# Adding Strassen sums to the residual by accumulating DMAs, in a transformer block on one Trainium2 core

## The chip, the core and the metric

The kernel runs on one NeuronCore of a Trainium2 chip. The core has five engines with an instruction queue each: TensorE (PE, matrix products; its weight loads are shown as PEld), VectorE (DVE), ScalarE (ACT), GpSimd (POOL) and SyncE (SP, which here only issues DMAs). An engine takes its instructions in order; what has to wait for another engine or for a DMA waits on a semaphore. Sixteen DMA engines carry all transfers. The metric is the device time of one execution in microseconds; it is the median of several runs.

## The reference, cut to what matters

One layer of an encoder block with four residual sub-blocks, each closed by a layer norm. 256 positions, 2048 features, everything in float32:

```python
h = layer_norm(ALPHA*h + 0.5*swiglu_ffn(h, ffn1_w_in, ffn1_w_out), ...)
h = layer_norm(ALPHA*h + hybrid_mixer(h, ...), ...)
h = layer_norm(ALPHA*h + memory_cross_attention(h, mem, ...), ...)
h = layer_norm(ALPHA*h + 0.5*swiglu_ffn(h, ffn2_w_in, ffn2_w_out), ...)
```

`ALPHA` is the fourth root of 2. The hidden width of an FFN is 5504. What matters here is the last product of a sub-block (`ffn1_w_out`, `w_xo`, `ffn2_w_out`), whose result, 256 x 2048, is added to `ALPHA*h`.

## The kernel before

**Arithmetic.** TensorE multiplies in a shorter float format. Each float32 operand is therefore split into a high plane (`hi`, ScalarE's copy, L264 for weights) and a remainder (`lo`, VectorE's subtraction, L267), and a product is the sum of three: high times high, remainder times high, high times remainder.

**Units.** Weights arrive in units of 1 MB in a `raw` buffer (three of them, loads issued by SP in L193, one by one as buffers come free). A unit holds two slices of 128 rows (contraction) of a group of 1024 output columns. `run` walks over a list of items; before an item's function is called it issues the loads and the splits (`load`, `halves`) of the units that come next, so the splits of later units stand ahead of the item's own instructions. Two pairs of `hi` and `lo` buffers exist.

**Groups.** `pair_group` computes 256 x 1024 outputs as 2 x 2 blocks of 128 x 512 in four PSUM banks `ps` (`mm` or `at`). A plain unit (`mm_pair`, L311) takes 24 matmuls. Some units, those in `at`, are done as a Strassen step (`mm_sums`, L366): seven block products in place of eight, 21 matmuls. They need sums of the weight blocks (`weight_sums`, L248 and L250, VectorE), sums of the activation blocks (`forms_step`, `sum_forms`, L321 and L325, VectorE), and four more banks `qs`. After the last such unit `shared` (the method, L679 to L684) combines the four banks into four sums of 128 x 512 in SBUF, tiles `w` (`w2`, six buffers, used by many steps): two copies on ScalarE and four additions on VectorE.

**Output groups.** `out_pair` is a group whose result goes to the residual `h`, two tiles of 128 x 2048. Right behind the method `shared`, its own inner function `shared` adds the four sums to `h`, on VectorE, with `ALPHA` multiplied in (L629) in the groups with `scale`, and without (L631) in the others. After the last unit `finish` adds the four banks `ps` (L754) and, where `st` is given, takes the layer norm's statistics of each piece (L390).

Seven output groups have Strassen steps: in ffn1 and in ffn2 each two of the first half of the hidden width (twelve units, Strassen steps in units 3, 5, 7 and 9, with `scale`) and one of the second half (ten units, the last a short one, steps in 3, 5 and 7, without `scale`, with statistics), and one in cross attention (eight units, steps in 2, 4 and 6, with `scale` and statistics). The remaining output columns are done by `out_proj` (L298) without Strassen steps. The two output groups of the mixer have none either; there `at` is empty and `finish` scales.

**Order.** `collect` gathers a stage's items into a list and `weave` puts side steps ahead of the list's entries by their position. In the first half of an FFN the side steps are: 2 the transposing DMAs of the last hidden block, 4 the sum forms of unit 7, 6 the return of that hidden block and the sum forms of unit 9. In cross attention: 1 the outputs of the last two heads and the forms of unit 2, 2 the forms of unit 4, 4 the forms of unit 6. Within this order the framework's scheduler decides how the instructions stand on each engine, by priority and readiness.

**GpSimd's queue** carries a few small loads: the gate bias rows (L912), the relative bias (L1048), rotation tables, the norm's gain and bias rows (L459, L460), the memory tokens (L1340, L1342).

Of the kernel before, what the change touches and what calls it, by code (L numbers as in the profile page):

```python
# [14 lines left out]
ALU = mybir.AluOpType  # L15
# [26 lines left out]
SUM_HOME = ("X2", "X3"),  # L42
# [5 lines left out]
ALPHA = 2.0 ** 0.25  # L48
# [53 lines left out]
class Kernel:  # L102
# [513 lines left out]
            turn = None  # L616
            f0 += nf

    def out_pair(self, bank, src, g, nk, x, at, fx, scale, st, sums_in=SUM_HOME):

        nc, h = self.nc, self.h
        ps, qs = {}, {}

        def shared():
            for (tt, a), s in qs["add"].items():
                c = (2 * g + a) * 512
                hs = h[tt][:, c:c + 512]
                if scale:
                    nc.vector.scalar_tensor_tensor(hs, hs, ALPHA, s, ALU.mult, ALU.add)  # L629
                else:  # L630
                    nc.vector.tensor_tensor(hs, hs, s, ALU.add)  # L631

        def finish():
            for tt in range(2):
                for a in range(2):
                    self.finish(tt, 2 * g + a, ps[tt, a], scale and not at, st)
        self.pair_group(bank, src, 512, nk, x, at, fx, ps, qs, shared, sums_in)
        self.add(finish)

    def group_tile(self, j):  # L640
# [1136 lines left out]
```

## Time and profile before

| | |
|---|---|
| median of 3 runs | 2434.71 us (2432.69 to 2434.84) |
| profiled execution, its time | 2432.52 us |
| profiled execution, its span | 2430.7 us |
| granted TensorE clock | 1.0 |
| instructions | 29702 |

A row of instructions reads: line of the kernel, engine, operation, output tile and input tiles (buffer numbers left out), shapes, and count. Where a row begins with two numbers, they are the start in the span and the duration, both in microseconds, and merged instructions of one kind carry a count (`x3`). Where it ends in three numbers with slashes, these are minimum, median and maximum of one instruction in nanoseconds. Rows of stretches give the busy time of each engine between two moments of the span, the number of instructions in brackets, then the clock, the share of the DMA engines' time and GB/s. DMA rows give the size of one transfer and the median time from its issue to its landing. Matmuls overlap one another, so a matmul's duration is longer than its share of TensorE's time.

### The profile page before, as it was taken

The page shows a single profiled execution, that of the slowest core. Times are in us where ns is not written, and L with a number is a line of the kernel's source. Part 1 is how long each engine was busy: PE and PEld are TensorE (multiplying, and loading weights), DVE is VectorE, ACT ScalarE, POOL GpSimd, SP SyncE. Part 2 cuts the span into 40 slices and gives each one's busy share as a digit, 9 for nine tenths or more (in the row PEclk, how much of TensorE's full clock was granted, in tenths as well). Part 3 has the DMA queues.
Part 4 walks back from the last instruction along what each step waited for, and adds up shares of the span by engine and source line. Part 5 has one row for each costly group of instructions (what it writes and reads, how often), then busy time and mean ns, then how long its engine had stood idle before and what let it go on. Part 6 is the DMA issues. An engine that isn't in the chain of part 4 may idle for free.

```text
span 2430.7 us, 29702 instructions
## 1 busy us (share of the span) xinstructions
PE 2422.3 (100%) x11280; PEld 2022.8 (83%) x11280; DVE 2130.9 (88%) x2437; ACT 1553.2 (64%) x2022; POOL 35.9 (1%) x81
## 2 busy tenths in 40 slices
PE   9999999999999999999999999999999999999999
PEld 8888888888888888888888888888888888888887
DVE  8999989899889998779788889979879999888997
ACT  6676745666555557878565687765666675556662
POOL 0000000000000001000000000000000000000000
PEclk9999999999999999999999999999999999999999
DMA  7766656667656657776577577655556766666665
GB/s 268 252 212 214 207 200 222 210 201 219 224 176 215 216 195 248 229 210 176 183 246 256 167 241 213 220 181 192 190 199 214 229 221 210 220 207 207 200 220 182
DMA packets 176414, 516.20 MB, mean 212 GB/s; under 512 B 111728, under 2 KB 112496, under 8 KB 121104
## 3 DMA queue, kind: packets, MB, share of 16 engines
q1 hardware_dynamic: 170816, 495.83, 61.6%
q0 software_dynamic: 4592, 17.30, 2.2%
q8 instruction: 88, 1.44, 0.2%
q10 hardware_dynamic: 864, 1.18, 0.1%
q14 instruction: 54, 0.44, 0.1%
HBM read 485.30 MB, written 2.10 MB: 201 GB/s over the span
## 4 chain that ended last, share of the span: by engine, by line
PE 89%; DVE 4%; ACT 3%; DMA 1%; issue 1%; SPq 0%; DVEq 0%; ACTq 0%
PE at L311 24%; PE mm L311 23%; PE at L366 11%; PE mm L366 11%; PE mm L298 10%; PE mm L277 4%; PE mm L279 2%; DVE lo L267 2%; ACT hi L264 1%; PE at L1034 1%; PE at L1505 0%; PE at L277 0%; DMA raw<-w_xv 0%; PE at L1088 0%; ACT H L854 0%
## 5 line engine op out<-in xcount | busy, mean ns | idle before, releaser
L264 ACT CAST hi<-raw 128x1024 fp32r<-128x1024 f32 (+1 forms) x852 | 804.0, 981 | 458.0 <-PE at L311 150.1
L267 DVE TENSOR_TENSOR lo<-raw,hi 128x2048 fp32r<-128x2048 f32 (+1 forms) x427 | 902.0, 2114 | 134.8 <-ACT hi L264 129.0
L311 PE MATMUL mm<-hi,T 128*128 128x512 f32 (+1 forms) x1312 | 307.5, 384 | 0.8 <-DVE v L400 0.7
L311 PEld LDWEIGHTS mm<-hi,T 128*128 128x128 f32 x1312 | 244.5, 188 | 46.9 <-DVE v L400 1.1
L264 ACT CAST X<-H 128x1024 fp32r<-128x1024 f32 (+1 forms) x170 | 174.8, 1035 | 160.9 <-DVE H L248 119.9
L311 PE MATMUL at<-hi,T 128*128 128x512 f32 x1136 | 272.3, 390 | 0.0
L311 PEld LDWEIGHTS at<-hi,T 128*128 128x128 f32 x1136 | 213.3, 188 | 44.5
L267 DVE TENSOR_TENSOR X<-H,X 128x2048 fp32r<-128x2048 f32 (+1 forms) x85 | 191.4, 2252 | 64.7 <-ACT X L264 64.7
L311 PE MATMUL mm<-lo,T 128*128 128x512 f32 (+1 forms) x656 | 158.4, 383 | 0.0
L311 PE MATMUL at<-lo,T 128*128 128x512 f32 x568 | 141.0, 389 | 0.0
L311 PEld LDWEIGHTS mm<-lo,T 128*128 128x128 f32 x656 | 122.3, 188 | 22.4
L311 PE MATMUL at<-hi,H 128*128 128x512 f32 x560 | 133.8, 390 | 0.0
L311 PEld LDWEIGHTS at<-lo,T 128*128 128x128 f32 x568 | 106.7, 188 | 22.1
L311 PEld LDWEIGHTS at<-hi,H 128*128 128x128 f32 x560 | 105.0, 188 | 21.5
L250 DVE TENSOR_TENSOR H<-H,raw 128x512 f32<-128x512 f32 (+1 forms) x170 | 115.4, 679 | 2.2
L311 PE MATMUL mm<-hi,H 128*128 128x512 f32 x480 | 115.5, 392 | 0.1
L311 PEld LDWEIGHTS mm<-hi,H 128*128 128x128 f32 x480 | 89.6, 188 | 18.9 <-DVE w L684 0.5
L248 DVE TENSOR_TENSOR H<-raw 128x1024 f32<-128x1024 f32 (+1 forms) x85 | 102.1, 1201 | 0.6 <-DMA raw<-w_gate 0.4
L366 PE MATMUL mm<-X,X 128*128 128x512 f32 x342 | 91.4, 393 | 0.0
L264 ACT CAST X<-raw 128x1024 fp32r<-128x1024 f32 (+1 forms) x54 | 55.4, 1035 | 47.9 <-DVE raw L250 38.6
L366 PE MATMUL at<-X,X 128*128 128x512 f32 (+1 forms) x315 | 82.6, 386 | 0.7 <-ACT X L264 0.7
L854 ACT COPY w<-w 128x1024 uint16<-128x1024 uint16 (+1 forms) x60 | 75.7, 1275 | 1.4 <-DMA w<-w 1.4
(387 smaller groups left out, 4151.3 us busy)
## 6 DMA issues: line engine op xcount, KB each, us to landing
raw<-ffn_w_in SPq DMA_DIRECT2D x150, 1024.0 KB, 4.9
raw<-ffn_w_out SPq DMA_DIRECT2D x66, 1024.0 KB, 4.9
raw<-w_gate SPq DMA_DIRECT2D x32, 1024.0 KB, 4.8
raw<-ffn_w_out_r SPq DMA_DIRECT2D x16, 1024.0 KB, 4.9
raw<-w_qk SPq DMA_DIRECT2D x16, 1024.0 KB, 5.6
raw<-w_o_b SPq DMA_DIRECT2D x16, 1024.0 KB, 4.8
raw<-w_out SPq DMA_DIRECT2D x16, 1024.0 KB, 5.0
raw<-w_xk SPq DMA_DIRECT2D x16, 1024.0 KB, 5.4
```

The source lines that it names most:

```text
L248: self.nc.vector.tensor_tensor(two[0], two[1], raw[:, :m].unsqueeze(1).to_broadcast([P, 2, m]), ALU.add)
L250: self.nc.vector.tensor_tensor(t[:, a * m:a * m + m], t[:, b * m:b * m + m], raw[:, a * m:a * m + m], ALU.add)
L264: self.last_hi = self.nc.scalar.copy(hi[:, c:d], src[:, c:d])
L267: self.last_lo = self.nc.vector.tensor_tensor(lo[:, :n], src, hi[:, :n].bitcast(F32), ALU.subtract)
L277: self.nc.tensor.matmul(ps, hi[j], x.both(kt), start=(j == 0), stop=False)
L279: self.last_mm = self.nc.tensor.matmul(ps[:, :S], lo[j], x.at(0, kt), start=False, stop=(j == n - 1))
L298: self.last_mm = self.nc.tensor.matmul(ps, x.at(xi, kt)[:, tt * P:(tt + 1) * P], w[wi][:, j * 512 + c:j * 512 + c + m], start=(start and j ...
L311: self.last_mm = self.nc.tensor.matmul(ps[tt, g][:, :n], x.at(xi, kt)[:, tt * P:(tt + 1) * P], w[wi][:, c:c + n], start=first and j + wi + ...
L366: self.last_mm = self.nc.tensor.matmul(bank[:, :m], a[xi], v[wi][:, c * m:(c + 1) * m], start=own and first and wi + xi == 0, stop=own and ...
L854: self.nc.scalar.copy(self.words(u, n).rearrange("p (c k) -> p k c", k=2), self.words(s, n).rearrange("p (k c) -> p k c", k=2))
L1034: nc.tensor.matmul(ps[:, c0:c0 + nk], q[:, tt * P:(tt + 1) * P], k[:, :nk], start=(j == 0), stop=(j == len(parts) - 1))
```

## The change

Only `out_pair` is changed. Its inner function `shared` no longer adds on VectorE: for each of the four sums GpSimd issues a DMA that adds the sum, tile `w`, to its part of `h` in SBUF (`accum_op=ALU.add`). Since a DMA cannot scale here, a new step `scaled` multiplies both tiles of `h`, the group's 1024 columns, by `ALPHA` on ScalarE, in the groups with `scale` and Strassen steps. The step is woven in at position 2 of the group's own list, ahead of unit 2. `finish` is unchanged; its additions read what the DMAs have written.

```diff
-    def out_pair(self, bank, src, g, nk, x, at, fx, scale, st, sums_in=SUM_HOME):
+    def out_pair(self, bank, src, g, nk, x, at, fx, scale, st, sums_in=SUM_HOME, order=None):
...
+        def scaled():
+            for tt in range(2):
+                hs = h[tt][:, g * 1024:(g + 1) * 1024]
+                nc.scalar.mul(hs, hs, ALPHA)
 
         def shared():
             for (tt, a), s in qs["add"].items():
                 c = (2 * g + a) * 512
-                hs = h[tt][:, c:c + 512]
-                if scale:
-                    nc.vector.scalar_tensor_tensor(hs, hs, ALPHA, s, ALU.mult, ALU.add)
-                else:
-                    nc.vector.tensor_tensor(hs, hs, s, ALU.add)
+                nc.gpsimd.dma_start(h[tt][:, c:c + 512], s, accum_op=ALU.add)
...
-        self.pair_group(bank, src, 512, nk, x, at, fx, ps, qs, shared, sums_in)
+        main = self.collect(lambda: self.pair_group(bank, src, 512, nk, x, at, fx, ps, qs, shared, sums_in, order))
+        self.weave(main, {2: [scaled]} if scale and at else {}, prio=0)
         self.add(finish)
```

No caller passes the new argument `order`, so it stays at `None`. The new step is an entry of its own in the list into which the callers weave their side steps by position: in the lists that begin with such a group, positions from 3 on now mean one unit less than before.

## The prediction

> **What bounds the kernel now.** I read the head of the page first, then the chain of waits, then the stretches around the seven places that the change touches, then the single instructions there.
>
> ```profile
> span 2430.7 us, 29702 instructions
> PE 2422.3 (100%) x11280; PEld 2022.8 (83%) x11280; DVE 2130.9 (88%) x2437; ACT 1553.2 (64%) x2022; POOL 35.9 (1%) x81
> PE 89%; DVE 4%; ACT 3%; DMA 1%; issue 1%; SPq 0%; DVEq 0%; ACTq 0%
> ```
>
> TensorE is busy for 2422.3 of 2430.7 us and makes up 89% of the chain that ends last; VectorE is behind it with 88% of the span. Idle time of TensorE is 8.4 us in all. A stage where TensorE works without a break cannot be shortened by lighter VectorE work, so the next view is busy time by stretch: one around the end of the Strassen sums of each of the seven output groups concerned (ffn1 three, cross attention one, ffn2 three), and two where the new ScalarE work would come.
>
> ```profile
> core 0: us, PE busy (x) PEld busy (x) DVE busy (x) ACT busy (x) POOL busy (x), PEclk, DMA share, GB/s
> 297.00:327.00 30.00, 30.00 (x134) 24.87 (x133) 26.06 (x24) 14.61 (x17) 0.00 (x0) 1.00 0.59 211
> 360.00:390.00 30.00, 30.00 (x134) 24.88 (x133) 27.62 (x35) 15.27 (x18) 0.00 (x0) 1.00 0.68 241
> 612.00:642.00 30.00, 30.00 (x134) 24.88 (x133) 27.19 (x29) 14.54 (x17) 0.00 (x0) 1.00 0.58 191
> 1668.00:1704.00 36.00, 36.00 (x160) 29.46 (x159) 35.56 (x46) 19.56 (x24) 0.00 (x0) 1.00 0.57 201
> 2038.00:2068.00 30.00, 30.00 (x135) 24.84 (x134) 27.37 (x27) 15.58 (x18) 0.00 (x0) 1.00 0.63 217
> 2103.00:2133.00 30.00, 30.00 (x134) 24.87 (x133) 28.80 (x35) 16.12 (x19) 0.00 (x0) 1.00 0.62 221
> 2352.00:2382.00 30.00, 30.00 (x134) 24.88 (x133) 26.48 (x29) 14.15 (x15) 0.00 (x0) 1.00 0.63 208
> 1650.00:1680.00 30.00, 30.00 (x155) 25.40 (x154) 29.48 (x43) 18.34 (x31) 0.00 (x0) 1.00 0.45 157
> 265.00:300.00 35.00, 35.00 (x156) 29.00 (x155) 34.46 (x36) 23.58 (x27) 0.00 (x0) 1.00 0.64 209
> ```
>
> The second number after the stretch is its length, the third TensorE's busy time: they are equal in all nine rows, and the granted clock is 1.00. VectorE is nearly full (35.56 of 36.00 at cross attention) and ScalarE about half busy, but neither makes TensorE wait there. What the change takes from VectorE was already hidden, so the whole question is whether what it adds stays hidden too.
>
> **The change part by part.**
>
> ```profile
> L629 DVE SCALAR_TENSOR_TENSOR h<-h,w x20: 682/684/693, 307.2 to 2115.0; 128x512 f32<-128x512 f32 x20
> L631 DVE TENSOR_TENSOR h<-h,w x8: 683/685/686, 624.7 to 2366.4; 128x512 f32<-128x512 f32 x8
> L924 ACT ACTIVATE H<-H x8: 1052/1062/1065, 773.6 to 902.1; 128x1024 f32<-128x1024 f32 x8
> L459 POOL DMA_DIRECT2D w<-gb x12: 536/536/548, 1069.6 to 1992.4; - x12
> ```
>
> Removed: 20 scaled adds of 0.684 us and 8 plain adds of 0.685 us, 13.7 + 5.5 = 19.2 us of VectorE, 2.7 us per group. On the path that sets the end this is 0, because TensorE has no gap in any of the seven stretches. If that cover were gone (VectorE late at a group's end), a group could give back at most its 2.7 us.
>
> Added on ScalarE: five of the seven groups scale (two each in the first halves of ffn1 and ffn2, one in cross attention), two multiplications each, in all ten of 128x1024. The nearest row is the 128x1024 activation of L924, 1.06 us: 10.6 us in all, 2.1 us per group, put ahead of the group's unit 2. The path sees them only if they make a weight split late. For the first group of ffn1 that slack can be read:
>
> ```profile
> 271.72 2.29 DVE L267 TENSOR_TENSOR X<-raw,X 128x2048 fp32r<-128x2048 f32 x1
> 276.80 0.84 PE L366 MATMUL at<-X,X 128*128 128x512 f32 x3
> ```
>
> The remainder plane of the summed weights is ready at 271.72 + 2.29 = 274.01 and first read at 276.80: 2.8 us early, against 2.1 us of new ScalarE work ahead of it in the worst case. So 0 on the path, between a gain of 0 (nothing is removed from ScalarE) and a loss of 2.1 us for a group whose slack is less.
>
> Moved: the scaling is one more entry in the group's list of steps, so what is woven in by position behind it comes one weight unit earlier: in the first halves of ffn1 and ffn2 the sum forms of unit 7 (position 4), and the return of the last hidden block with the forms of unit 9 (position 6); in cross attention the forms of unit 6 (position 4). This is the same work about 5 us sooner, on a VectorE that is full at 265 to 300 and 1650 to 1680 us. Nothing that it reads is late. I take 0 for its mean, from −0.5 to +2 us for each of the three places, the upper end being again a ScalarE share of about 2.1 us put in a wrong place.
>
> Added on GpSimd's queue: 28 DMAs. At 0.536 us an issue that is 15.0 us, 2.1 us per group, on an engine that shows no instruction in any of the nine stretches; its other transfers (the gb rows, the mask and bias loads) lie outside them, so nothing is queued behind. SP's queue with the weight loads gets no new instruction.
>
> Added wait: the group's finishing adds (L754) read what the DMAs write, so on VectorE they wait for the landing, and everything behind them in VectorE's order (statistics L390, then the next weights' remainder, L267) waits too. An accumulating DMA stands nowhere in this trace. The nearest rows are GpSimd's other transfers, from issue to landing:
>
> ```profile
> w<-gb POOLq DMA_DIRECT2D x24, 256.0 KB, 4.2
> X<-gate_row POOLq DMA_DIRECT2D x4, 512.0 KB, 5.8
> H<-memT POOLq DMA_DIRECT2D x1, 1024.0 KB, 8.0
> T<-rope POOLq DMA_DIRECT2D x1, 256.0 KB, 2.8
> DMA to landing us min/median/max: 3.3/4.2/7.2
> ```
>
> One sum is 256 KB; the last row is of the 24 gb transfers alone. Below, 2.8 us, the quickest transfer of that size; above, 8.0 us, the slowest of a megabyte, which is all four sums of a group in flight at once. I take 5.8 us, the row of 512 KB, since an addition must read the target as well as the source. The Trainium skill, "Collectives: The Full Stack", section "The bandwidth ceiling", says that an add in the DMA needs two source reads and goes at about half the rate of a copy; by that the landing would be that of 512 KB, which is the value above, and no run so far shows it.
>
> How late may a landing be? Cross attention is the tightest, since one unit of weights stands between its last sum and its finish:
>
> ```profile
> 1695.61 0.68 DVE L684 TENSOR_TENSOR w<-w,mm 128x512 f32<-128x512 f32 x1
> 1696.20 1.89 DVE L629 SCALAR_TENSOR_TENSOR h<-h,w 128x512 f32<-128x512 f32 x3
> 1698.01 2.28 DVE L267 TENSOR_TENSOR lo<-raw,hi 128x2048 fp32r<-128x2048 f32 x1
> 1702.60 1.26 DVE L754 TENSOR_TENSOR h<-h,at 128x512 f32<-128x512 f32 x2
> 1703.79 1.27 DVE L390 BATCH_NORM_STATS2 bn<-h 128x6 f32<-128x512 f32 x2
> 1704.99 2.27 DVE L267 TENSOR_TENSOR lo<-raw,hi 128x2048 fp32r<-128x2048 f32 x1
> 1709.58 1.07 PE L298 MATMUL mm<-lo,X 128*128 128x512 f32 x4
> ```
>
> The last sum is ready at 1695.61 + 0.68 = 1696.3, in the changed kernel about 0.6 us sooner, 1695.7, because the first scaled add no longer stands ahead of it. Behind its landing come one finishing add (0.6 us at the spacing of these rows), two statistics (1.2) and a remainder (2.3), and TensorE reads that remainder at 1709.58. So the landing may take 1709.58 − 1695.7 − 4.1 = 9.8 us. In the second halves of the two FFNs the second sum decides:
>
> ```profile
> 624.14 0.69 DVE L682 TENSOR_TENSOR w<-w,w 128x512 f32<-128x512 f32 x1
> 630.55 1.28 DVE L754 TENSOR_TENSOR h<-h,at 128x512 f32<-128x512 f32 x2
> 631.86 2.29 DVE L267 TENSOR_TENSOR lo<-raw,hi 128x2048 fp32r<-128x2048 f32 x1
> 637.74 1.07 PE L298 MATMUL mm<-lo,H 128*128 128x512 f32 x4
> ```
>
> It is ready at 624.8; behind its landing stand 0.6 us of finishing add and 2.3 us of remainder, read at 637.74, which leaves 10.0 us. The four groups of the first halves have two whole units behind the last sum and so more room. Taken at 5.8 us, or at the upper end of 8.0 us, the wait is covered everywhere: VectorE may stand for some microseconds at L754, but it no longer does the 2.7 us of adds, and TensorE does not notice. If that cover is gone, each further microsecond of landing costs one microsecond in three groups.
>
> **Sum.** 0 (adds) + 0 to 2 (scaling and moved steps, of which I take 0.5 for the crowded stretches at 265 and 1650 us) + 0 (issues) + 0 (landings) = 0.5 us on the profiled execution. That execution took 2432.5 us, a span of 2430.7 and 1.8 us around it; the median of the runs is 2434.7, 2.2 us above. Forecast: 2433.0 for that execution, 2435.2 as a median. A difference under 0.2%, 4.9 us, is what a measurement of this kernel hardly tells from no change.
>
> **The rivals.**
>
> *Late landings (slower).* Four sums in flight together beside the weight loads land later than 10 us after they are ready, and VectorE, which takes its instructions in order, stands at L754 with the remainder of the next weights behind it. For: the DMA engines are already 57 to 63% busy in the three tight stretches, and the accumulation is unseen here. Against: a whole megabyte landed in 8.0 us at worst. The price is (L − 9.8) + 2 × (L − 10.0): it passes 4.9 us at L = 11.6, and at L = 15 it is 15 us, 2450. A second way to the same end: GpSimd cannot write descriptors while VectorE works, so that each issue lasts until a VectorE instruction ends, up to 2.3 us; four issues then take 9.2 instead of 2.1 us, and the last landing goes from 5.8 to 12.9 us after the sum, at a price of 3.1 us in cross attention and, since its second sum is delayed by one or two issues only, nothing sure in the others. Against it, 0.536 us is minimum and median of the issue row, on a VectorE that is busy nine tenths of the time. The Trainium skill, "SBUF — State Buffer", section "SBUF: two separate sides", has this as a trap: an issue of 620 ns becomes about 3100 ns beside a VectorE instruction that holds the shared port pair. By that figure four issues would take 12.4 us; the issue row above does not show it. 0.13 for late landings, 0.02 for slow issues.
>
> *Crowded ScalarE (slightly slower).* The 2.1 us of scaling and the steps moved forward meet in the stretches at 265 and 1650 us and the same place of ffn2, where VectorE has under 2% left, and the splits come late by more than the 2.8 us of slack. Price at most 2.1 + 2 us in each of three places less that slack, about 1.3 × 3 = 4 us: 2439, with a tail to 2442. For: VectorE 34.46 of 35.00. Against: ScalarE has 11.4 us free in the same row. 0.12, of which 0.06 passes 0.2%.
>
> *VectorE was the hidden bound (faster).* The 19.2 us freed lets weights be split sooner everywhere behind the groups, and TensorE's idle time goes. Its price is bounded by that idle time: 8.4 us at most, so 2426 to 2430. Against: none of that idle time lies in the nine stretches. 0.06.
>
> *The forecast*, nothing moves: 0.67.
>
> **How the numbers follow.** The predicted time is that of the forecast, 2435.2. Slower by over 0.2%: 0.13 + 0.02 + 0.06 = 0.21. Faster by over 0.2%: 0.06. Within: 0.67 + 0.06 = 0.73. The forecast's own range is 2432 to 2438 (the runs shown span 2432.7 to 2434.8, and the additions 0 to 2 us with the moved steps between −1.5 and +6 at their ends). The range for 8 in 10 reaches up into the crowded case and the start of the late landings, and a little below the forecast's: 2431 to 2444.
>
> **What would show it.** In the changed profile VectorE should be some 19 us less busy, ScalarE 10 to 11 us more, and GpSimd should have 28 issues of about 0.54 us. TensorE's busy time should fill the same seven stretches. L754 should show a wait for the DMAs, of a few microseconds at cross attention and in the two second halves, and no weight load of TensorE should have that behind it. A landing over 10 us, an issue over 1 us, or new TensorE gaps behind L754 would make the forecast wrong on the slow side; fewer TensorE gaps far from the groups, on the fast side.

## The result: 4.6 us slower, most of it in cross attention

The changed kernel takes 2439.28 us as a median of 20 runs (2433.22 to 2445.14), the kernel before beside it 2434.64 us (2432.69 to 2437.14, 20 runs). The ratio is 1.0018, 95% interval 1.0011 to 1.0025: 4.6 us slower, just under the 0.2% (4.9 us) that the prediction took as the bound of what can be told, but with 20 runs each the interval leaves out 1. The runs also spread over 12 us instead of 4.5. The profiled execution of the changed kernel was a quick one, 2434.94 us. Three executions in the experiments below (two of all but cross attention, one of the kernel before) took 3017 us or more and are left out of the figures.

The head of its page (span, busy time of each engine) and the shares by engine of the chain that ended last:

```profile
span 2433.1 us, 29768 instructions
PE 2422.8 (100%) x11280; PEld 2021.0 (83%) x11280; DVE 2115.9 (87%) x2409; ACT 1561.6 (64%) x2032; POOL 60.4 (2%) x109
PE 81%; DVE 6%; issue 6%; ACT 3%; DMA 3%; SPq 0%; DVEq 0%; POOL 0%; ACTq 0%; POOLq 0%
```

VectorE is 15.0 us less busy (2130.9 to 2115.9), ScalarE 8.4 us more, GpSimd 24.5 us more, and TensorE's work is what it was. In the chain TensorE's share falls from 89% to 81%; what comes in is VectorE (4 to 6%), DMA (1 to 3%) and time in which a row shows no releaser (1 to 6%).

Busy time by stretch, columns as in the prediction: a group of a first half, cross attention, and the layer norm's transposes behind it:

```profile
core 0: us, PE busy (x) PEld busy (x) DVE busy (x) ACT busy (x) POOL busy (x), PEclk, DMA share, GB/s
297.00:327.00 30.00, 30.00 (x134) 24.82 (x134) 23.27 (x20) 15.14 (x17) 3.65 (x4) 1.00 0.79 246
...
1668.00:1704.00 36.00, 36.00 (x159) 29.23 (x158) 32.05 (x39) 19.40 (x25) 3.52 (x4) 1.00 0.68 206
...
1736.00:1744.00 8.00, 7.45 (x42) 6.08 (x41) 6.10 (x20) 5.15 (x10) 0.00 (x0) 1.00 0.39 160
```

The groups' own stretches are still full (30.00 of 30.00, 36.00 of 36.00), as forecast. The DMA engines are busier there, 0.79 after 0.59. TensorE loses 0.55 us in a stretch that the prediction did not look at, the norm behind cross attention, where it was busy for 8.00 of 8.00 us before. The new transfers in the same execution, duration of the issue on GpSimd and, last, time from issue to landing:

```profile
L632 POOL DMA_DIRECT2D h<-w x28: 853/888/1330, 306.3 to 2367.0; - x28
...
  DVE h L756: 6.9, 6
  DVE w L325: 3.3, 2
...
DMA to landing us min/median/max: 5.5/7.9/11.1
```

A transfer lands after 7.9 us, up to 11.1, not after 5.8. The finishing additions (now L756) stand 6.9 us for them in six waits, three of which, 3.3 us in all, are in cross attention. A second wait was not thought of: L325 (sum forms) stands 3.3 us, because the tiles `w` that the DMAs read come free only at the landing.

Cross attention in this execution, from VectorE's last combination of the sums (L686) to TensorE's first use of the remainder plane behind the finish (times as in the rows of the prediction; in brackets the idle time before an instruction and what ended it):

```profile
1696.56 0.68 DVE L686 TENSOR_TENSOR w<-w,mm 128x512 f32<-128x512 f32 x1
...
1703.60 0.69 DVE L756 TENSOR_TENSOR h<-h,at 128x512 f32<-128x512 f32 x1 [1.46 <-DMA h<-w]
1704.86 0.69 DVE L756 TENSOR_TENSOR h<-h,at 128x512 f32<-128x512 f32 x1 [0.57 <-DMA h<-w]
1706.66 0.67 DVE L756 TENSOR_TENSOR h<-h,at 128x512 f32<-128x512 f32 x1
1707.97 2.28 DVE L267 TENSOR_TENSOR lo<-raw,hi 128x2048 fp32r<-128x2048 f32 x1
...
1710.43 0.86 PE L298 MATMUL mm<-lo,X 128*128 128x512 f32 x3
```

The last finishing addition begins 9.4 us after the last sum (1706.66 − 1697.24), the plane is ready at 1710.25 and is read at 1710.43: covered, with 0.2 us to spare. In a slower execution the same rows read differently; that is the first experiment.

### The profile page after: what moved, and what is told of

It reads as the page before. It is cut to its first block, busy times and chain, and to the rows that moved or that the text cites. A ratio compares the mean times of both kernels' runs of the same rounds, so it can differ in the third digit from the quotient of the medians.

```text
span 2433.1 us, 29768 instructions
## 1 busy us (share of the span) xinstructions
PE 2422.8 (100%) x11280; PEld 2021.0 (83%) x11280; DVE 2115.9 (87%) x2409; ACT 1561.6 (64%) x2032; POOL 60.4 (2%) x109
## 4 chain that ended last, share of the span: by engine, by line
PE 81%; DVE 6%; issue 6%; ACT 3%; DMA 3%; SPq 0%; DVEq 0%; POOL 0%; ACTq 0%; POOLq 0%
PE at L311 22%; PE mm L311 21%; PE at L366 10%; PE mm L366 10%; PE mm L298 9%; PE mm L277 4%; DVE lo L267 3%; PE mm L279 2%; ACT hi L264 1%; PE at L1036 1%; DMA raw<-w_xq 1%; DMA raw<-ffn_w_in 1%; DMA raw<-w_xo_r 1%; PE at L1090 0%; PE at L277 0%
## 5 line engine op out<-in xcount | busy, mean ns | idle before, releaser
L267 DVE TENSOR_TENSOR lo<-raw,hi 128x2048 fp32r<-128x2048 f32 (+1 forms) x427 | 901.9, 2113 | 141.3 <-ACT hi L264 135.1
L267 DVE TENSOR_TENSOR X<-H,X 128x2048 fp32r<-128x2048 f32 (+1 forms) x85 | 191.4, 2252 | 59.4 <-ACT X L264 59.4
L366 PEld LDWEIGHTS mm<-X,X 128*128 128x128 f32 x342 | 63.6, 188 | 14.8 <-DVE X L267 1.5
```

The source lines that it names most:

```text
L267: self.last_lo = self.nc.vector.tensor_tensor(lo[:, :n], src, hi[:, :n].bitcast(F32), ALU.subtract)
L366: self.last_mm = self.nc.tensor.matmul(bank[:, :m], a[xi], v[wi][:, c * m:(c + 1) * m], start=own and first and wi + xi == 0, stop=own and ...
```

## The experiments

Four theories stood against one another. W: the wait of the finishing additions for the landing, with a weight plane behind it. T: the added DMA traffic delays weight loads, in proportion to the transfers. O: the change moved other instructions in the scheduler's order. S: the scaling on ScalarE and the steps moved forward. Each run was timed in five rounds beside the kernel before. "Lag in cross attention" is worked out from the traces: the start of the same matmul in both kernels, its difference to the profile of before at 1800 us less that at 1690 us. For the quick execution of the changed kernel it is 1.68 − 0.69 = 1.0 us.

**The changed kernel again** (no edit).

> The changed kernel once more, unedited, to see in a second profile where a slower execution than the first profiled one (2434.9 us, near the fastest of its runs) loses time. Every theory expects +4 to +5 us over the kernel before (2434.6), with runs spread over some 10 us. Theory W (the wait): the finishing adds L756 stand on VectorE until the accumulating DMAs land, and in the slower runs TensorE has gaps within 10 us behind cross attention (about 1700 us) and the two second halves (630, 2370 us). Theory T (traffic): the sums share the DMA engines with the weight loads; the gaps are waits of ScalarE for raw loads, behind all seven groups. Theory O (order): the gaps are spread over the whole kernel, also far from the groups, where the scheduler put VectorE's instructions in another order; TensorE gaps near 507, 1307, 1738, 2206 and 2248 us come back at the same places.

2438.97 us, ratio 1.0024 (1.0013 to 1.0035); the profiled execution took 2438.32 us, and 3.7 of the 5.8 us by which its span is longer than that of before are the lag in cross attention. The same rows:

```profile
1698.28 0.68 DVE L686 TENSOR_TENSOR w<-w,mm 128x512 f32<-128x512 f32 x1
...
1705.81 0.69 DVE L756 TENSOR_TENSOR h<-h,at 128x512 f32<-128x512 f32 x1 [2.39 <-DMA h<-w]
1707.08 0.69 DVE L756 TENSOR_TENSOR h<-h,at 128x512 f32<-128x512 f32 x1 [0.58 <-DMA h<-w]
...
1711.08 0.69 DVE L756 TENSOR_TENSOR h<-h,at 128x512 f32<-128x512 f32 x1 [2.11 <-DMA h<-w]
1712.41 2.27 DVE L267 TENSOR_TENSOR lo<-raw,hi 128x2048 fp32r<-128x2048 f32 x1
...
1714.74 1.20 PE L298 MATMUL mm<-lo,X 128*128 128x512 f32 x4 [2.41 <-DVE lo L267]
```

The last sum is ready at 1698.96 and its addition begins at 1711.08: 12.1 us, 2.3 over the limit of 9.8 that the prediction had worked out. TensorE stands 2.41 us, and the row names the plane behind the wait. Only the last of the four transfers is that late, 11.8 us from issue to landing, after 8.6 in the quick execution: the same code on either side of one limit, which is where the wider spread can come from.

**The scaling alone.** ScalarE scales, VectorE adds the sums, no DMA.

```diff
-                nc.gpsimd.dma_start(h[tt][:, c:c + 512], s, accum_op=ALU.add)
+                hs = h[tt][:, c:c + 512]
+                nc.vector.tensor_tensor(hs, hs, s, ALU.add)
```

> The scaling step on ScalarE at position 2 stays, with the steps that it moves forward, and the sums are added by VectorE as before (plain adds in all seven groups): no DMA. Theory S (scaling and moved steps cost): +4 to +5 us over the kernel before. Theories W and T: no change, within 1.5 us of the kernel before. Theory O: little, 0 to 2 us, since only some 50 instructions of VectorE stand elsewhere than before, against some 150 in the changed kernel.

2433.03 us, ratio 0.9999 (0.999 to 1.0007): S falls. One small thing stays: TensorE's transposes of the norm behind cross attention (L421) wait 0.7 us for VectorE here too, without any DMA, and the lag in cross attention is 1.0 us, as much as in the quick execution of the changed kernel.

**Sums into other columns**, so that no finishing addition waits.

```diff
-                c = (2 * g + a) * 512
+                c = (2 * (1 - g) + a) * 512
```

> The same 28 accumulating DMAs at the same places, but each group's sums are added to the other 1024 columns of h, which nothing reads until 30 us or more later: the finishing adds of the group no longer wait for them. The sums land in the wrong columns; the work is the same. Theory W: back to the kernel before, within 1.5 us. Theory T: still +4 to +5 us. Theory O: still +3 to +5 us, since the order on all engines is nearly that of the changed kernel (17 instructions of VectorE differ). Theory S: still +4 to +5 us.

2449.08 us, ratio 1.0062 (1.0049 to 1.0076): every expectation missed. Its table of waits (who waits for what: us in total, times, longest) shows why:

```profile
ACT h L627 <- DMA h<-w: 19.6, 4, 5.6
```

The scaling of the other group now waited for the DMAs, 19.6 us in four places, and ScalarE's weight copies behind it. It tells nothing of W or T, but shows once more what a landing costs at the head of an in-order queue.

**The same, mended:** all columns are scaled in the first group's step, so that nothing on ScalarE waits either.

```diff
-                hs = h[tt][:, g * 1024:(g + 1) * 1024]
-                nc.scalar.mul(hs, hs, ALPHA)
+                for k in ((0, 1) if st is None else (g,)):
+                    hs = h[tt][:, k * 1024:(k + 1) * 1024]
+                    nc.scalar.mul(hs, hs, ALPHA)
...
-                c = (2 * g + a) * 512
+                c = (2 * (1 - g) + a) * 512
...
-        self.weave(main, {2: [scaled]} if scale and at else {}, prio=0)
+        self.weave(main, {2: [scaled]} if scale and at and g == 0 else {}, prio=0)
```

> The same 28 accumulating DMAs at the same times, but into the columns of the other half of the residual, which no finishing addition reads soon; all columns are scaled in the first group's step, so that no ScalarE instruction waits for a landing either. The output is then not the reference's. If the wait at the finishing addition is the cost (W): no DMA is named before L756, and the time falls to 0 to 2 us over before (what moved steps cost). If the DMA traffic beside the weight loads is the cost (T) or the GpSimd issues: it stays 4 to 5 us over before. If the order of instructions is the cost (O): also 3 to 5 us over, with the small TensorE gaps where the changed kernel has them.

2436.1 us beside 2433.7, ratio 1.0012 (1.0003 to 1.002), no DMA named before L757 (the finishing additions here), lag in cross attention 1.0 us and no gap near 1711. The median is 2.4 us over, a little more than W allows and about half of what T and O ask. So the wait is some half of the loss by this run, and the interval is too wide to say more.

**The first halves alone** (four groups by DMA, the others by VectorE).

```diff
-                nc.gpsimd.dma_start(h[tt][:, c:c + 512], s, accum_op=ALU.add)
+                hs = h[tt][:, c:c + 512]
+                if st is None:
+                    nc.gpsimd.dma_start(hs, s, accum_op=ALU.add)
+                elif scale:
+                    nc.vector.scalar_tensor_tensor(hs, hs, ALPHA, s, ALU.mult, ALU.add)
+                else:
+                    nc.vector.tensor_tensor(hs, hs, s, ALU.add)
```

> DMAs and scaling only in the four groups of the FFNs' first halves, which have two units of weights behind the last sum; cross attention and the two second halves add on VectorE as before. Theory W: back to the kernel before, within 1.5 us, since the three groups with little room no longer wait. Theory T: four of seven groups are left, about +2.6 us. Theory O: +3 to +5 us, since the order up to cross attention and in ffn2 is that of the changed kernel. Theory S: +3 to +5 us.

2436.51 us, ratio 1.0009 (1.0 to 1.0017). Alone this looks like half of the loss; the next two runs correct it.

**Cross attention alone, and all but cross attention.** The same edit with the condition `st is not None and scale`, and with its opposite.

> Only cross attention's four sums go by accumulating DMA, with their scaling; the six groups of the feed-forward parts are as before. W: 2 to 3 us over before, with a TensorE gap near 1710 us in slower executions. T (spread evenly over the 28 DMAs): 0.7 us over. O: 0 to 1 us over.

> The opposite: the 24 DMAs of the feed-forward parts, with their scaling, cross attention as before. W: about 2 us over before, that is about the loss measured with the first halves alone (2.3 us), since the landings of the second halves are under their limit of 10 us; no gap near 1710. T: 4 us over. O: 3 to 4 us over.

Cross attention alone: 2438.77 us, ratio 1.0017 (1.0008 to 1.0026), lag there 4.0 us. Everything else, 24 of the 28 transfers: 2434.71 us, ratio 1.0001 (0.9991 to 1.001), lag 0.0; that is below W's 2 us, too. So four transfers cost about what all 28 cost, and a cost in proportion to them (T) falls. W's number for cross attention (2 to 3 us) was too small; the trace has two gaps, not one. First the timeline of cross attention alone, then its table of waits from 1696 to 1745 us:

```profile
1697.19 0.68 DVE L692 TENSOR_TENSOR w<-w,mm 128x512 f32<-128x512 f32 x1
...
1709.29 0.69 DVE L762 TENSOR_TENSOR h<-h,at 128x512 f32<-128x512 f32 x1 [1.65 <-DMA h<-w]
1710.62 2.27 DVE L267 TENSOR_TENSOR lo<-raw,hi 128x2048 fp32r<-128x2048 f32 x1
...
1712.95 1.19 PE L298 MATMUL mm<-lo,X 128*128 128x512 f32 x4 [1.73 <-DVE lo L267]
```

```profile
ACT T L264 <- DMA raw<-w_xo_r: 8.9, 2, 4.5
...
PE at L421 <- DVE h L413: 1.6, 1, 1.6
```

The landing, 11.4 us after the last sum, costs 1.73 us by the limit. Then VectorE is late with the norm, too, and TensorE stands another 1.6 us at the transposes, where the scaling alone has 0.7. How much of this second gap comes from the late additions, and how much from the weight loads, for which ScalarE waits 8.9 us here (first row of the table) and 4.3 us in the kernel before, this run does not separate. The first-halves run, which shares 16 transfers with the second of these, is to be read with its interval, which reaches down to 1.0.

**The same 28 transfers as plain copies.**

```diff
-                nc.gpsimd.dma_start(h[tt][:, c:c + 512], s, accum_op=ALU.add)
+                nc.gpsimd.dma_start(h[tt][:, c:c + 512], s)
```

> The same 28 DMAs to the same places at the same times as plain copies that overwrite the residual's columns; the addition is left out, so the output is not the reference's. If reading the target as well makes the accumulating DMA long: landings fall from 7.9 to about 4 us, issues from 0.85 to 1.3 us back to about 0.54 us; W then gives 0 to 2 us over before, O 3 to 5 us. If four transfers in flight beside the weight loads make it long: landings stay at 7 to 8 us, issues at 0.9 us or more, and the time at 4 to 5 us over before by every theory.

2432.77 us, ratio 0.9997 (0.9988 to 1.0005). Order, scaling, waits and bytes are those of the changed kernel; only the addition is gone, and with it the loss: O falls. (W and T are not told apart here, since the landing and the engines' time shrink together.) The transfers' rows, as above:

```profile
L632 POOL DMA_DIRECT2D h<-w x28: 536/538/709, 306.3 to 2363.9; - x28
...
  DVE h L756: 1.2, 1
...
DMA to landing us min/median/max: 4.0/5.3/9.0
```

Landing 5.3 instead of 7.9 us (about 4 was expected), in cross attention 4.5 us for the last of the four, issue 0.538 instead of 0.888 us, the wait at L756 1.2 instead of 6.9 us, and no loss. The queue of GpSimd's transfers (packets, MB, share of the 16 engines' span), in the kernel before, the changed one and this one:

```profile
q0 software_dynamic: 4592, 17.30, 2.2%
```

```profile
q0 software_dynamic: 8624, 24.65, 3.9%
```

```profile
q0 software_dynamic: 6832, 24.65, 3.0%
```

For the same 7.35 MB the additions take 144 packets each (4032 by 28) and 1.7% of the engines' span, the copies 80 and 0.8%. The Trainium skill, "Collectives: The Full Stack", section "The bandwidth ceiling", has a ReduceScatter, in which the DMA engines add, at about half the rate of an AllGather, in which they copy, because an add needs two source reads. The share of the engines' span here agrees with that (1.7 to 0.8), while the landing grows only by half (7.9 to 5.3).

**The finish of cross attention moved back**, behind the remainder plane of the unit after the next; all 28 additions stay.

```diff
+        if st is not None and scale and at:
+            return finish
         self.add(finish)
...
+            def after_planes():
+                with self.tc.issue_after(self.last_lo.ins):
+                    late()
+            self.weave(rest, {1: [after_planes]}, prio=0)
```

(`late` is the returned `finish`, `rest` the items of `out_proj`.)

> All 28 accumulating DMAs and the scaling stay; only the finishing additions of cross attention stand later in VectorE's order, behind the remainder plane of the weight unit after the next, so that a landing of about 12 us after the last sum does not hold a plane that TensorE needs soon. Nothing is left out. If the wait in cross attention is the cost (W): the TensorE gap near 1711 us goes and the time falls to 0 to 1.5 us over before, no faster than before. If the DMA traffic (T) or the order elsewhere (O) is the cost: it stays 4 to 5 us over before.

2435.54 us, ratio 1.0009 (1.0 to 1.0017), 1.7 us over before by the medians: a little above W's 0 to 1.5, well below the 4 to 5 of T and O. About half of the loss goes. The gap near 1711 is gone, but the wait has moved. From the table of waits, 1696 to 1745 us:

```profile
ACT H L264 <- DMA raw<-w_xo_r: 6.4, 2, 5.2
...
PE at L421 <- DVE h L413: 1.6, 1, 1.6
```

Additions and statistics that stand later make VectorE late for the norm, and TensorE waits there, 1.6 us at L421; the lag in cross attention is 2.0 us. So moving the wait does not remove it.

**Each sum of cross attention sent twice** (on the edit of cross attention alone, `for _ in range(2):` ahead of the DMA).

> As in the run with cross attention alone, but each of its four sums is sent twice, so that the sums count double in the output; the feed-forward parts are as before. At 0.9 to 1.3 us an issue the last issue starts some 4 us later. W: the last landing goes from 11 us to some 15 to 17 us after the last sum, and each microsecond over 9.8 costs one: 8 to 11 us over before, with TensorE gaps of 6 us or more in all between 1705 and 1745 us. T, at the 1.0 us for each DMA that the four of cross attention cost there (4.1 us by four): also 8 us over, but spread, without one large gap behind L762.

2446.3 us, ratio 1.0051 (1.0037 to 1.0065), 12.5 us over before, and 11.2 us of it is the lag in cross attention. The timeline there:

```profile
1697.62 0.68 DVE L693 TENSOR_TENSOR w<-w,mm 128x512 f32<-128x512 f32 x1
...
1716.37 0.69 DVE L763 TENSOR_TENSOR h<-h,at 128x512 f32<-128x512 f32 x1 [0.63 <-DMA h<-w]
1718.17 2.27 DVE L267 TENSOR_TENSOR lo<-raw,hi 128x2048 fp32r<-128x2048 f32 x1
...
1720.50 2.08 PE L298 MATMUL mm<-lo,X 128*128 128x512 f32 x4 [7.63 <-DVE lo L267]
```

One large gap behind the wait, as W asks and T does not: 18.1 us from the last sum to its addition, 8.3 over the limit, and 7.63 us of standing, with 0.93 us at an earlier plane. The last landing was later than the 15 to 17 us expected, since GpSimd itself waited 5.6 us for the first addition to the same columns before it issued the second, and another 3.8 us for which the trace names no cause. The two gaps are 8.56 of the 11.2 us of lag. About 2.0 us more is a slower TensorE: its granted clock is 0.50 from 1720.5 to 1724.0 us, and the first twelve matmuls behind the long gap take 4.70 us, where twelve take 2.73 us before it. So this gap cost more than its length.

**Cross attention alone, into other columns.**

> Only cross attention's four sums go by accumulating DMA, at the same times, but into columns 1024 to 2047, which out_proj's additions read some 20 us later; the sums then stand in the wrong columns of the output. W: no wait at the group's finishing additions, no gap near 1711 us, 0 to 1 us over before, against 4.1 us with the wait. T: 4 us over, as with the wait.

2435.45 us, ratio 1.0007 (0.9998 to 1.0016), 1.6 us over before by the medians: a little over W's 0 to 1, far from T's 4. The lag is 1.4 us against 4.0 with the wait, and 1.0 with the scaling alone. So with the same four transfers, at the same times, the median is 3.3 us lower when nothing waits for them. No gap near 1711; what is left stands at the transposes (table of waits, 1696 to 1745 us):

```profile
ACT T L264 <- DMA raw<-w_xo_r: 5.0, 1, 5.0
...
PE at L421 <- DVE h L413: 0.6, 1, 0.6
```

The weight loads beside the additions land after up to 8.7 us (6.7 before), and SP issues the sixth of them at 1716.8 us (1711.7 before). That is T's share, but the 0.6 us at L421 are also in the run without any DMA, so no gap is shown to come from it.

**Two of the four sums.**

```diff
+                mixed = st is not None and scale
+                if mixed and tt == 0:
+                    nc.gpsimd.dma_start(hs, s, accum_op=ALU.add)
+                elif scale and not mixed:
```

> As the run with cross attention alone, but only two of its four sums, those of the first row tile, go by accumulating DMA; the other two are added by VectorE (plain additions, the scaling stays on ScalarE). Nothing is left out. With two transfers instead of four behind the last sum, the last landing should come about 8 us after its sum, below the limit of 9.8 us. Cost by a limit (W, late landings): no TensorE gap near 1711 us and 0 to 1 us over before. Cost in proportion to the transfers (T): half of the 4.1 us of four, 2 us over before; eight cost 12.5 us.

2436.34 us beside 2433.4, ratio 1.001 (1.0001 to 1.0019). The median is 2.9 us over, above W's 0 to 1 and nearer to T's 2, and the interval (0.2 to 4.6 us) excludes neither. The trace speaks for the limit: the last awaited landing comes 6.4 us after the last sum, TensorE does not stand near 1711, and the lag in cross attention is 0.5 us. The margin is small, though: behind this addition stand two more additions and four statistics, so the limit for it is 6.7 us and not 9.8. Where this execution lost time is elsewhere, most of all at the norm behind ffn1, where the kernel's code is as before: TensorE stands 2.1 us there up to 681.85 us, its granted clock is 0.50 from 682 to 685 us, and the lag grows by some 3.5 us between 640 and 700 us. What the 2.9 us of the median are made of, stays open.

**Limit and loss in one table** (from the end of L686, or its like, to the start of the last finishing addition that reads what a DMA wrote; the excess over 9.8 us; the idle time in TensorE's row at the plane behind it):

| | us | excess | stands |
|---|---|---|---|
| two sums | 6.4 | 0 | 0 |
| changed, quick execution | 9.4 | 0 | 0 |
| cross attention alone | 11.4 | 1.6 | 1.73 |
| changed, again | 12.1 | 2.3 | 2.41 |
| each sum twice | 18.1 | 8.3 | 7.63 (+0.93) |

## Why the prediction was right, and which terms were off

The time lies in the stated range, 2431 to 2444, but outside the forecast's own, 2432 to 2438. All three signs that the prediction named for a forecast wrong on the slow side came: a landing over 10 us (11.8), an issue over 1 us (1.33), and a TensorE gap behind the finishing additions (2.41 us, in the slower execution).

*VectorE relieved: 0.* Held. 15.0 us less on VectorE bought nothing: with plain copies, all the relief and none of the late landings, the ratio is 0.9997. (15.0 and not 19.2, in part since the adds overlap back to back: three took 1.89 us, not 2.05. That makes 17.6; the rest was not traced.)

*Scaling and moved steps: 0.5 us.* Held as a bound for the whole: 0.9999 for the scaling alone, though its trace has 1.0 us of lag in cross attention. The crowding at 265 and 1650 us did not come; the first scaling ran at 96.4 us, some 170 us ahead of its group's stretch, since the scheduler had set it that far ahead in ScalarE's order.

*Issues: 0.536 us each, 0 on the path.* The size was wrong, 0.888 us as a median and up to 1.33: an accumulating DMA takes longer to issue than a plain one, which the plain copies show (0.538) beside the same VectorE work. The slow-issue rival, issues that last until a VectorE instruction ends, is thereby excluded as the reason: in cross attention four issues took 3.5 us, not 9.2.

*Landing: 5.8 us, from 2.8 to 8.0.* This is the step that failed. The median was 7.9 us, and the last of the four in cross attention took 8.6, 11.1 and 11.8 us in three executions, past the upper end. The 8.0 us of a whole megabyte did not bound four additions of 256 KB: it was the row of a copy.

*The limit: 9.8 us in cross attention, 10.0 us in the second halves, one microsecond for each beyond.* The limit in cross attention held, to about 0.1 us in the two cases of one clear gap, but partly by luck. The last sum came later against TensorE's work than reckoned: the first use of the plane stands only 13.2 to 13.4 us behind it instead of 13.9, the waiting left out. But only one statistic stands behind the last addition instead of two, so that the plane is ready 3.6 us after the addition begins, not 4.1. The two errors nearly cancel. The second halves did not cross it in the profiled execution (slowest landing from issue 9.2 us), and all but cross attention has the ratio 1.0001. So the rival "late landings" was right in its mechanism and in one of its three places, at 11.4 to 12.1 us after the sum. Its price was too small there: with cross attention alone a second gap came behind the plane's, 1.6 us at the norm's transposes, which the formula did not have. (The 0.6 us there in the changed kernel run again are no more than the 0.7 of the scaling alone.)

*The sum.* 2435.2 forecast, 2439.3 measured, in the range and within 0.2%, but not for the reason given (nothing moves): that the number is so near is owed to a small loss, not to the working. Of the 4.6 us, about 4.1 (0.0017 by 2434) can be laid to cross attention by its own run; the remainder is within the intervals. The traces also have a small effect of order: in four groups that the change does not touch (at 508, 1505, 2207 and 2249 us) TensorE waits 1.3 us in all for L686 (0.7 and 0.6 in the table of waits), where before shows no such wait. In three of them a remainder (L267) now stands ahead of the last combinations. The plain copies have 0.5 us of these waits, at no loss that could be measured.

## What to carry to other kernels

Taking work off an engine that does not bound the kernel is worth nothing, while the way back, a landing, can bound it: price a moved addition by the slowest landing of the last transfer, not by the median of a plain one. Work out the limit per place (when is the first thing behind the wait needed?) and compare it with that slowest landing; of seven places the one with the least room held, by the ratios, nearly all of the loss. Do not take a gap of TensorE at its length alone: twice here a slower clock behind it added to the price. When a wait near its limit is pushed back, look at what next needs the engine: here the layer norm did.

## What the runs showed of the hardware

An accumulating DMA of 256 KB between SBUF tiles took 0.888 us to issue and 7.9 us to land (5.5 to 11.1), a plain copy of the same 0.538 and 5.3 us (4.0 to 9.0). It took 144 packets instead of 80 and about twice the engines' time. The last of four in flight varied from 8.6 to 11.8 us between executions of one program.

TensorE's granted clock fell to 0.50 for some 3 us behind gaps of 7.63 us (each sum twice) and 2.10 us (two sums), and stayed at 1.00 behind one of 2.41 us (the changed kernel again). So the length of the gap alone did not decide it.
